# Copying the rows of a key and value cache inside DRAM, instead of storing them from the tiles that were loaded for the attention

## The chip, the cores and the metric

The kernel is one program on one NeuronCore of one Trainium2 chip. The metric is device time in microseconds (us); a row of the profile is one execution of that program as the hardware profiler saw it. The engines are called as the profile calls them: PE (TensorE, matmuls), PEld (its weight loads), DVE (VectorE), ACT (ScalarE), POOL (GpSimd), SP (SyncE). SP, ACT and POOL issue DMAs, each on a ring of its own (q1, q10 and q0 in the profile); all rings are served by the same 16 DMA engines. SPq is SP's queue as an issuer of DMAs.

## The reference, cut to what matters

One inference step of one decoder layer: a prompt of 1024 tokens and, beside it, 8 sequences of 8 new tokens each with a cache of 2048 rows of keys and values (8 heads of 64, so 512 floats or 2 KB a row). A mixer of two head groups (gated DeltaNet and windowed attention) is followed by a SwiGLU FFN. For the 8 sequences, the attention reads the cache and the step also returns the cache moved on by 8 rows:

```python
def token_mix(h, conv_buf, s0, win_k, win_v, ...):
    proj = h @ w_in
    ...
        n_past = win_k.shape[1]                                    # 2048
        kc = jnp.concatenate([win_k.astype(kb.dtype), kb], axis=1)
        vc = jnp.concatenate([win_v.astype(vb.dtype), vb], axis=1)
        parts = [dilated_branch_sample(qf, kcf, vcf, slopes, d, w // d, n_past) for (w, d) in DILATED]
        keep = min(MAX_WINDOW, n_past + T)                         # 2048
        new_k, new_v = kc[:, n_past + T - keep:], vc[:, n_past + T - keep:]
    o_b = rmsnorm(combine_by_denominator(parts), norm_out_b)
    mixed = jnp.concatenate([o_a.reshape(B, T, A_WIDTH), o_b.reshape(B, T, B_WIDTH)], axis=-1)
    return mixed @ w_out, new_conv, s_new, new_k, new_v

def hybrid_block(x, ...):
    mix, new_conv, new_rec, new_k, new_v = token_mix(rmsnorm(x, norm_mix), ...)
    x = x + mix
    hf = rmsnorm(x, norm_ffn)
    x = x + (jax.nn.silu(hf @ w_gate) * (hf @ w_up)) @ w_down
```

So `new_wk_sample[b, 0:2040] = cache_win_k[b, 8:2048]`, its last 8 rows are the new keys, and the same holds for V. That is 2040 rows of 2 KB for each of 8 sequences, for K and for V. The attention itself reads only a part of the cache: with a dilation of 16 the first eight of every 16 rows of rows 0 to 1535, and all of the last 512 rows.

## The kernel before

All matmuls of the dense parts are made exact by splitting both operands into a high and a low part, so each weight block costs three matmuls. A weight block of 128 x 1024 floats is loaded by SP into `wraw` (two buffers, `WB`), ACT copies the high part into `whi`, DVE takes the low part into `wlo` (three buffers each, `WH` and `WL`; `wsplit` and `split`, L216 to L233).

The program is written as Python generators that record the work of a stage and yield a cost; `beside` (L1384) takes from a main stage and, by a pace given as a number, from one or two stages beside it. The Tile framework then schedules the recorded instructions for each engine by their dependences and priorities, so an engine's final order differs from the order of recording; each engine runs its own order and waits on semaphores. `tc.keep_in_program_order` pins an instruction to its recorded place.

The stages in order: the projection `proj_a` of both halves of the prompt with the DeltaNet `gdn` beside it (its small block copies into `N1` run on POOL, L650 and L651), `proj_b` with the first half of `decode_k` (`dk`, attention scores of the 8 sequences against the cached keys) beside it, the attention of the prompt `attn(0)` and the output projection `outproj_a`; then the dense work of the first half of the prompt (`outproj_b(0)`, `ffn(0)`) with `attn(1)`, the second half of `decode_k` and then `decode_v` beside it; last `out1` and `ffn(1)` for the second half.

`decode_k` works on pairs of sequences. For each sequence it loads the last 512 rows in two tiles `kt` of 512 KB (L1021; transposed by PE, copied to `kaT` by ACT, multiplied with the query block `qbd`), and the 16-dilated rows in four tiles of 384 KB (L1037; multiplied on DVE with a broadcast query `qbc`, the product `pr`, L994). `kt` has three buffers. `decode_v` loads the values likewise into `vt` (four buffers, L1104) and splits them into `vh` and `vl`. In both, each loaded tile is stored from SBUF into the moved cache by a DMA that POOL issues (L1022, L1038, L1107, L1109):

```python
sp.dma_start(kt[:96], c16[:96, t:t + 2])
pool_q.dma_start(o16[0:95, 8 + t:10 + t], kt[1:96])
scores(S[:, s, t * 8:t * 8 + 16], kt[:96], q[:96], 96)
```

A buffer of `kt` or `vt` may be loaded anew only when its store has landed. The rows that the attention doesn't read (the second eight of every 16) are copied inside DRAM by `far_rows`, one DMA of 96 pieces of 16 KB (1536 KB) for each sequence, on SP's queue, pinned to its recorded place: for K beside `proj_b(0)`, for V beside `out1` and `ffn(1)`.

Of the kernel before, what the change touches and what calls it, by code (L numbers as in the profile page):

```python
# [22 lines left out]
DB, DS = 8, 8  # L23
PAST = 2048
# [7 lines left out]
R1 = 2.0  # L32
# [5 lines left out]
R7 = 1.4  # L38
# [7 lines left out]
U3 = 120  # L46
# [94 lines left out]
def body(tc, I, O, C, off):  # L141
# [843 lines left out]
    def decode_k(tp, pairs, kb=2, kt_=3, qb=2, pb=1):  # L985
# [23 lines left out]
        for pi in pairs:  # L1009
            S = tp.tile([96, 2, 64], F32, name="S", tag="S", bufs=1)  # L1010
            pa = obank()
            for s in range(2):
# [6 lines left out]
                for r in range(0, 4, 2):  # L1019
                    kbt = tp.tile([128, 2, 512], F32, name="kt", tag="kt", bufs=kt_)  # L1020
                    sp.dma_start(kbt, c4[:, r:r + 2])  # L1021
                    pool_q.dma_start(o4[:, r:r + 2], kbt)  # L1022
                    for q in range(2):
                        p_ = nbank()
                        for j in range(4):
                            pe.transpose(p_[:, j * 128:(j + 1) * 128], kbt[:, q, j * 128:(j + 1) * 128], ident)
                        kaT = tp.tile([128, 4, 128], F32, name="kaT", bufs=kb)
                        act.activation(kaT, p_.rearrange("p (j m) -> p j m", j=4), AF.Copy)
                        for j in range(4):
                            mm(pa[s * 64:(s + 1) * 64, (r + q) * 128:(r + q + 1) * 128], qbd[:, s, j], kaT[:, j],  # L1030
                               j == 0, j == 3)
                    yield 4.0
                for t in range(0, 8, 2):
# [4 lines left out]
                    pool_q.dma_start(o16[0:95, 8 + t:10 + t], kt[1:96])  # L1038
# [19 lines left out]
    def decode_v(tp):  # L1058
# [10 lines left out]
        for pi in range(4):  # L1069
# [17 lines left out]
            for s in range(2):  # L1087
# [11 lines left out]
                for i in range(6):  # L1099
# [6 lines left out]
                    if i < 4:  # L1106
                        pool_q.dma_start(o16[0:95, 8 + 2 * i:10 + 2 * i], vt[1:96])  # L1107
                    else:
                        pool_q.dma_start(o4[:, 2 * i - 8:2 * i - 6], vt)  # L1109
# [228 lines left out]
    def far_rows(c, o, new):  # L1338

        for b in range(DB):  # L1340
            c16, o16, *_ = cache_rows(c, o, b)
            tc.keep_in_program_order(sp.dma_start(o16[0:96, 0:8], c16[0:96, 8:16]))
            yield 4.5
# [91 lines left out]
    far = Side(far_rows(I["cache_win_k"], O["new_wk_sample"], smp[1]))  # L1435
    beside(Side(proj_a(1, tpa, tp, *acts1)), (gd, R0))
    tst2.close()
    beside(Side(proj_b(0, tp, *acts0)), (gd, R1), (far, 0.3))
    far.run()
# [29 lines left out]
    with ExitStack() as s1:  # L1469
        at1 = Side(attn(1, pool(s1, "at", "right"), **A1), ahead=O4)  # L1470
        beside(dense, (at1, R7), until=U3)
        at1.run()
    pst.close()
# [17 lines left out]
    far = Side(far_rows(I["cache_win_v"], O["new_wv_sample"], smp[2]))  # L1491
    beside(out1, (far, 0.3))
    beside(Side(ffn(1, op, x2, hp)), (far, 0.3))
# [28 lines left out]
```

## Time and profile before

| what | value |
|---|---|
| time, median of 3 runs | 1830.91 us (1815.8 to 1832.13) |
| profiled execution | 1808.45 us, of it 1806.7 us span from the first to the last instruction |
| mean granted clock of PE in it | 0.982 |
| busy share of the span | PE 95%, PEld 82%, DVE 64%, ACT 38%, POOL 5% |
| moved by DMA | 325.00 MB; on SP's ring 275.64 MB, on POOL's ring 43.08 MB |

The profiled execution lies 1.2% under the median of the runs, so changes are added up against its own time. The share of a busy engine is an average over stages: what a change is worth is read in the stage where it acts. A DMA share of 1 means that all 16 DMA engines were busy. A wait in brackets names what the engine was released by.

### The profile page before, as it was taken

What the parts mean: (1) busy time and instruction counts of PE and PEld (TensorE: products, weight loads), DVE (VectorE), ACT (ScalarE), POOL (GpSimd) and SP (SyncE); (2) the same over time, 40 slices, a digit from 0 to 9 for tenths busy, and PEclk for the clock granted to TensorE, in tenths of its full rate; (3) what the DMA queues carried; (4) which work ended last, traced back from release to release, by engine and by line L of the source; (5) the groups of instructions that cost most, each with busy time, mean ns of one, the idle gap of its engine ahead of it and who ended that gap; (6) DMA issues with size and microseconds to landing.
All of it is one profiled execution on the core that took longest, in us unless ns stands there. A gap on an engine that the chain in (4) does not pass through costs nothing. (4 is left out here: it accounts for less than half of the span.)

```text
span 1806.7 us, 28517 instructions
## 1 busy us (share of the span) xinstructions
PE 1716.0 (95%) x10718; PEld 1490.3 (82%) x10718; DVE 1151.8 (64%) x2829; ACT 695.3 (38%) x1411; POOL 84.7 (5%) x208
## 2 busy tenths in 40 slices
PE   6999999998999999999998899999997999999997
PEld 6988799987656668978977787788887999999996
DVE  7879776866775657897655556676576444353445
ACT  5545344442333444676422234444234222131222
POOL 0000000001001000000010201111100000000000
PEclk9999999999999999999999999999998999999999
DMA  6444555558987957633288859898395332241321
GB/s 204 130 141 129 152 192 142 176 180 278 294 246 250 284 172 240 211 103 104 79 265 247 258 159 325 250 293 275 123 330 171 132 103 82 59 130 38 112 71 64
DMA packets 305476, 325.00 MB, mean 180 GB/s; under 512 B 28349, under 2 KB 252605, under 8 KB 303786
## 3 DMA queue, kind: packets, MB, share of 16 engines
q1 hardware_dynamic: 291610, 275.64, 50.3%
q0 software_dynamic: 12352, 43.08, 6.9%
q10 hardware_dynamic: 1376, 4.46, 0.6%
q8 instruction: 84, 1.38, 0.3%
q14 instruction: 54, 0.44, 0.1%
HBM read 242.92 MB, written 105.63 MB: 193 GB/s over the span
## 5 line engine op out<-in xcount | busy, mean ns | idle before, releaser
L192 PE MATMUL pm<-act_hi,whi 128*128 128x288 f32 (+1 forms) x1056 | 351.4, 333 | 0.7 <-DVE hth L1294 0.4
L192 PE MATMUL pm<-act_lo,whi 128*128 128x288 f32 (+1 forms) x1056 | 350.8, 332 | 0.0
L192 PE MATMUL pm<-act_hi,wlo 128*128 128x288 f32 (+1 forms) x1056 | 349.5, 331 | 0.0
L217 ACT ACTIVATE whi<-wraw 128x1024 fp32r<-128x1024 f32 x182 | 192.9, 1060 | 354.0 <-PE pm L192 257.6
L218 DVE TENSOR_TENSOR wlo<-wraw,whi 128x1024 fp32r<-128x1024 f32 x182 | 222.4, 1222 | 120.0 <-ACT whi L217 119.4
L192 PE MATMUL pm<-xh,whi 128*128 128x320 f32 (+2 forms) x672 | 229.0, 341 | 4.6 <-DVE th L424 2.7
L192 PE MATMUL pm<-xh,wlo 128*128 128x320 f32 (+2 forms) x672 | 228.3, 340 | 0.6 <-DVE wlo L218 0.5
L192 PE MATMUL pm<-xl,whi 128*128 128x320 f32 (+2 forms) x672 | 227.7, 339 | 0.1
L192 PEld LDWEIGHTS pm<-act_hi,whi 128*128 128x128 f32 x1056 | 200.8, 190 | 17.5 <-issue 1.5
L192 PEld LDWEIGHTS pm<-act_lo,whi 128*128 128x128 f32 x1056 | 200.8, 190 | 15.3 <-issue 1.3
L192 PEld LDWEIGHTS pm<-act_hi,wlo 128*128 128x128 f32 x1056 | 200.7, 190 | 14.7 <-issue 0.7
L192 PEld LDWEIGHTS pm<-xh,whi 128*128 128x128 f32 x672 | 129.3, 192 | 16.2 <-DVE th L424 2.9
L1319 DVE TENSOR_TENSOR x<-pm,x 128x256 f32<-128x256 f32 (+1 forms) x148 | 79.9, 544 | 94.3 <-PE pm L192 93.9
L192 PEld LDWEIGHTS pm<-xh,wlo 128*128 128x128 f32 x672 | 129.0, 192 | 11.7 <-DVE wlo L218 1.6
L192 PEld LDWEIGHTS pm<-xl,whi 128*128 128x128 f32 x672 | 128.9, 192 | 11.5 <-issue 2.7
L192 PE MATMUL pm<-own,hh 128*128 128x512 f32 x440 | 129.4, 390 | 0.0
L192 PE MATMUL pm<-whi,hh 128*128 128x256 f32 (+1 forms) x336 | 99.3, 297 | 5.3 <-DVE x L1319 3.3
L192 PE MATMUL pm<-whi,hl 128*128 128x256 f32 (+1 forms) x336 | 97.4, 292 | 0.0
L192 PE MATMUL pm<-wlo,hh 128*128 128x256 f32 (+1 forms) x336 | 97.2, 290 | 0.0
L192 PEld LDWEIGHTS pm<-own,hh 128*128 128x128 f32 x440 | 82.2, 188 | 16.9 <-issue 0.2
L192 PE MATMUL pm<-whi,nat_hi 128*128 128x256 f32 x288 | 83.4, 294 | 2.0 <-DVE n_ss L213 1.1
L1292 ACT ACTIVATE hth<-pm 128x288 f32<-128x288 f32 (+1 forms) x66 | 30.5, 462 | 139.7 <-PE pm L192 139.7
(365 smaller groups left out, 3248.4 us busy)
## 6 DMA issues: line engine op xcount, KB each, us to landing
wraw<-w_in SPq DMA_DIRECT2D x56, 512.0 KB, 4.9
wraw<-w_gate SPq DMA_DIRECT2D x44, 512.0 KB, 4.2
wraw<-w_up SPq DMA_DIRECT2D x44, 512.0 KB, 3.7
wraw<-w_down SPq DMA_DIRECT2D x44, 512.0 KB, 3.7
new_wk_sample<-cache_win_k SPq DMA_DIRECT2D x8, 1536.0 KB, 9.1
qbc<-smp SPq DMA_DIRECT2D x32, 384.0 KB, 5.4
kt<-cache_win_k SPq DMA_DIRECT2D x32, 384.0 KB, 6.1
vt<-cache_win_v SPq DMA_DIRECT2D x32, 384.0 KB, 4.3
```

The lines of the kernel that those rows point to most:

```text
L192: pe.matmul(out, lhsT, rhs, start=start, stop=stop)
L217: act.activation(hi, src, AF.Copy)
L218: dve.tensor_sub(lo, src, hi.bitcast(F32))
L1292: act.activation(th, pg[:, :n], AF.Tanh, scale=0.5)
L1319: dve.tensor_tensor(xv, ps, xv, op=OP.add)
```

## The change

The four stores out of `kt` and `vt` are taken out of `decode_k` and `decode_v`. `far_rows` becomes `move_rows`: for each sequence two DMAs, from DRAM to DRAM, of 1020 consecutive rows each (2.09 MB), which together are all 2040 rows. They are issued on POOL's queue instead of SP's and are no longer pinned. K is recorded beside `proj_b(0)` and the dense work beside `attn(1)`, V beside `ffn(1)`. The loads for the attention stay as they are.

```diff
--- before.py
+++ after.py
@@ -1019,7 +1019,6 @@
                 for r in range(0, 4, 2):
                     kbt = tp.tile([128, 2, 512], F32, name="kt", tag="kt", bufs=kt_)
                     sp.dma_start(kbt, c4[:, r:r + 2])
-                    pool_q.dma_start(o4[:, r:r + 2], kbt)
                     for q in range(2):
                         p_ = nbank()
                         for j in range(4):
@@ -1035,7 +1034,6 @@
                     q_rows(q[:96], t, b, 96)
                     kt = tp.tile([128, 2, 512], F32, name="kt", tag="kt", bufs=kt_)
                     sp.dma_start(kt[:96], c16[:96, t:t + 2])
-                    pool_q.dma_start(o16[0:95, 8 + t:10 + t], kt[1:96])
                     scores(S[:, s, t * 8:t * 8 + 16], kt[:96], q[:96], 96)
                     yield 3.0
             p_ = nbank()
@@ -1103,10 +1101,6 @@
                     vl = tp.tile([128, 2, 512], F32R, name="vl", bufs=VB)
                     sp.dma_start(vt[:n], c16[:96, 2 * i:2 * i + 2] if i < 4 else c4[:, 2 * i - 8:2 * i - 6])
                     split(vh[:n], vl[:n], vt[:n])
-                    if i < 4:
-                        pool_q.dma_start(o16[0:95, 8 + 2 * i:10 + 2 * i], vt[1:96])
-                    else:
-                        pool_q.dma_start(o4[:, 2 * i - 8:2 * i - 6], vt)
                     for q in range(2):
                         mm(po, z[:n, 2 * i + q], vh[:n, q], i + q == 0, False)
                         mm(po, z[:n, 2 * i + q], vl[:n, q], False, False)
@@ -1335,12 +1329,15 @@
                         yield nb * ncol / 800
             f += nb
 
-    def far_rows(c, o, new):
-
+    def move_rows(c, o, new):
+
+        n = (PAST - DS) // 2
         for b in range(DB):
-            c16, o16, *_ = cache_rows(c, o, b)
-            tc.keep_in_program_order(sp.dma_start(o16[0:96, 0:8], c16[0:96, 8:16]))
-            yield 4.5
+            for q in range(2):
+                s_, d_ = (x[0, b, r:r + n].rearrange("(a e) h d -> a (e h d)", a=60) for x, r in
+                          ((c, DS + q * n), (o, q * n)))
+                pool_q.dma_start(d_, s_)
+                yield 4.5
         sp.dma_start(o[0, :, PAST - DS:PAST].rearrange("b t h d -> b t (h d)"), new.rearrange("(b t) f -> b t f", t=DS))
 
     def steps(*gens):
@@ -1432,11 +1429,10 @@
     nc.gpsimd.memset(Bz, 0.0)
     nc.gpsimd.memset(N1, 0.0)
     gd = Side(gdn(gp, Bz, N1), gdn_sample(gp), ahead=O1)
-    far = Side(far_rows(I["cache_win_k"], O["new_wk_sample"], smp[1]))
+    far = Side(move_rows(I["cache_win_k"], O["new_wk_sample"], smp[1]))
     beside(Side(proj_a(1, tpa, tp, *acts1)), (gd, R0))
     tst2.close()
-    beside(Side(proj_b(0, tp, *acts0)), (gd, R1), (far, 0.3))
-    far.run()
+    beside(Side(proj_b(0, tp, *acts0)), (gd, R1), (far, 0.2))
     es0.close()
     pst.close()
     psum(pst, m=2, n=2, g=2, c=1, o=1)
@@ -1468,8 +1464,9 @@
     dense = Side(outproj_b(0, hp, x2), ffn_norm(0, hp, x2), ffn(0, hp, x2, hp))
     with ExitStack() as s1:
         at1 = Side(attn(1, pool(s1, "at", "right"), **A1), ahead=O4)
-        beside(dense, (at1, R7), until=U3)
+        beside(dense, (at1, R7), (far, 0.25), until=U3)
         at1.run()
+        far.run()
     pst.close()
     psum(pst, **PSE)
     with ExitStack() as s1:
@@ -1488,9 +1485,9 @@
     pst.close()
     psum(pst, m=6, n=2)
     hp = pool(st0, "hh")
-    far = Side(far_rows(I["cache_win_v"], O["new_wv_sample"], smp[2]))
-    beside(out1, (far, 0.3))
-    beside(Side(ffn(1, op, x2, hp)), (far, 0.3))
+    far = Side(move_rows(I["cache_win_v"], O["new_wv_sample"], smp[2]))
+    beside(out1)
+    beside(Side(ffn(1, op, x2, hp)), (far, 0.22))
     far.run()
     st0.close()
     st1.close()
```

The program that is built from it has another order. At the start of the program, POOL's order was this (`gdn_S`, `Bz` and `N` are buffers of the DeltaNet, `N` is `N1` of the code):

```order
L1422 MEMSET gdn_S 128x512
L1432 MEMSET Bz 128x1024
L1433 MEMSET N_1431 128x512
L650 COPY N_1431<-L 32x4x32
L651 COPY N_1431<-L 32x4x32
```

Now there are copies between them:

```order
L1419 MEMSET gdn_S 128x512
L1339 DMA new_wk_sample<-cache_win_k 32x16320 x3
L1429 MEMSET Bz 128x1024
L1430 MEMSET N_1431 128x512
L1339 DMA new_wk_sample<-cache_win_k 32x16320 x3
L650 COPY N_1431<-L 32x4x32
L651 COPY N_1431<-L 32x4x32
L1339 DMA new_wk_sample<-cache_win_k 32x16320 x3
```

Nine of the 16 K copies stand at the first three places of POOL's order, recorded a stage or more later.

On POOL again, from the end of the first half of `decode_k` over `outproj_a` (`xq` is its residual tile) to the second half of `decode_k` (`qbd`), it was:

```order
L1038 DMA new_wk_sample<-kt 95x1024 x4
L1204 MEMSET xq 64x256 x2
L1055 DMA pd<-Pd 128x616
L1204 MEMSET xq 64x256 x2
L1007 MEMSET qbd 128x512
L1018 COPY qbd<-qf 64x8 x16
L1022 DMA new_wk_sample<-kt 128x1024 x2
```

And now:

```order
L1339 DMA new_wv_sample<-cache_win_v 32x16320 x2
L1198 MEMSET xq 64x256
L1339 DMA new_wv_sample<-cache_win_v 32x16320
L1053 DMA pd<-Pd 128x616
L1198 MEMSET xq 64x256 x2
L1339 DMA new_wv_sample<-cache_win_v 32x16320
L1198 MEMSET xq 64x256
L1339 DMA new_wv_sample<-cache_win_v 32x16320 x5
L1007 MEMSET qbd 128x512
L1018 COPY qbd<-qf 64x8 x32
```

The last V copy stands ahead of the second half of `decode_k`, two stages before the one in which it was recorded; the stores are gone from their places behind `qbd`.

On SP, at the entry into `out1` and `ffn(1)` (`wffn` is the norm's weight row), it was:

```order
L222 DMA wraw<-w_out 128x4x256 x2
L1342 DMA new_wv_sample<-cache_win_v 96x4096
L222 DMA wraw<-w_out 128x4x256
L294 DMA wffn<-norm_ffn 128x1024
L1342 DMA new_wv_sample<-cache_win_v 96x4096
L222 DMA wraw<-w_gate 128x8x128
L222 DMA wraw<-w_up 128x8x128
L1342 DMA new_wv_sample<-cache_win_v 96x4096 x2
```

And now:

```order
L222 DMA wraw<-w_out 128x4x256 x2
L294 DMA wffn<-norm_ffn 128x1024
L222 DMA wraw<-w_out 128x4x256
L222 DMA wraw<-w_gate 128x8x128
L222 DMA wraw<-w_up 128x8x128
```

The copies between the weight loads are gone from SP's order.

## Rows read from the trace of the kernel before

**Rows 1.** Page, busy time of each engine, share of the span and instructions

```profile
PE 1716.0 (95%) x10718; PEld 1490.3 (82%) x10718; DVE 1151.8 (64%) x2829; ACT 695.3 (38%) x1411; POOL 84.7 (5%) x208
```

**Rows 2.** Stretches: length, then busy us (instructions) by engine, granted clock, DMA share, GB/s

```profile
3.00:15.00 12.00, 4.11 (x17) 3.38 (x17) 8.30 (x26) 6.79 (x12) 0.00 (x0) 1.00 0.96 322
29.00:60.00 31.00, 31.00 (x224) 31.00 (x225) 29.59 (x83) 19.64 (x41) 1.42 (x2) 0.93 0.47 125
130.00:160.00 30.00, 30.00 (x173) 25.01 (x173) 27.03 (x104) 18.25 (x54) 0.57 (x2) 1.00 0.42 125
206.50:211.00 4.50, 2.91 (x25) 2.61 (x24) 2.99 (x7) 2.05 (x3) 0.00 (x0) 0.97 0.94 390
400.00:520.00 120.00, 108.33 (x624) 82.67 (x623) 86.83 (x230) 37.74 (x102) 11.63 (x32) 1.00 0.89 272
520.00:700.00 180.00, 174.86 (x968) 122.83 (x968) 110.62 (x315) 75.20 (x186) 11.81 (x33) 0.99 0.76 235
700.00:760.00 60.00, 56.17 (x424) 51.77 (x423) 45.70 (x118) 31.38 (x61) 0.31 (x1) 1.00 0.73 230
900.00:1060.00 160.00, 142.92 (x820) 120.85 (x820) 84.94 (x106) 37.72 (x52) 21.67 (x57) 0.96 0.81 242
1060.00:1300.00 240.00, 234.99 (x1277) 197.21 (x1276) 152.65 (x228) 102.39 (x139) 29.19 (x58) 0.99 0.79 250
1300.00:1400.00 100.00, 89.00 (x572) 80.61 (x571) 68.40 (x164) 37.42 (x58) 2.87 (x5) 0.91 0.68 239
```

**Rows 3.** Stretches at the lower clock between 900 and 1300, same columns

```profile
937.80:944.60 6.80, 5.80 (x17) 4.70 (x18) 3.58 (x4) 0.95 (x2) 0.52 (x1) 0.50 0.90 278
1036.80:1043.60 6.80, 3.01 (x10) 2.07 (x10) 4.20 (x5) 1.60 (x3) 0.38 (x1) 0.50 0.72 202
1118.70:1125.50 6.80, 5.81 (x13) 4.12 (x14) 5.12 (x5) 3.24 (x4) 1.05 (x2) 0.50 1.08 381
```

**Rows 4.** Waits of SP's DMA queue: us in total, times, longest us

```profile
SPq L1037 <- DMA new_wk_sample<-kt: 49.6, 15, 7.2
SPq L1104 <- DMA new_wv_sample<-vt: 48.1, 18, 5.2
```

**Rows 5.** Timeline around 1033: start us, us, engine, line, operation [idle before <-releaser]

```profile
1026.30 0.53 POOL L1038 DMA_DIRECT2D new_wk_sample<-kt  x1 [0.56 <-DMA kt<-cache_win_k]
...
1032.04 0.31 SPq L1037 DMA_DIRECT2D kt<-cache_win_k  x1
...
1036.23 1.22 DVE L994 TENSOR_TENSOR pr<-kt,qbc 96x1024 f32<-96x1024 f32 x1 [6.26 <-DMA kt<-cache_win_k]
...
1040.59 0.66 PE L192 MATMUL po<-kaT,qbd 128*64 128x128 f32 x2 [7.82 <-ACT kaT L1028]
```

**Rows 6.** Timeline of POOL, same columns

```profile
0.74 0.53 POOL L1422 MEMSET gdn_S<- 128x512 f32 x1 [0.29 <-POOLq L1513]
33.66 0.96 POOL L1432 MEMSET Bz<- 128x1024 f32 x1 [32.40 <-DVE n_ss L208]
...
138.56 0.28 POOL L650 COPY N<-L 32x128 f32<-32x128 f32 x1 [103.48 <-DVE L L556]
...
702.44 0.31 POOL L1204 MEMSET xq<- 64x256 f32 x1 [7.19 <-DMA k<-ks]
```

**Rows 7.** Timeline of the start, same columns

```profile
8.99 1.28 DVE L283 SCALAR_TENSOR_TENSOR xn<-xt,n_ss,wmix 128x1024 f32<-128x1024 f32 x1 [0.52 <-DMA wmix<-norm_mix]
...
10.50 1.06 ACT L217 ACTIVATE whi<-wraw 128x1024 fp32r<-128x1024 f32 x1 [3.50 <-DMA wraw<-w_in]
```

**Rows 8.** Instructions on y_prompt: time from DMA to landing

```profile
DMA to landing us min/median/max: 2.0/6.0/6.0
```

**Rows 9.** Old copies into new_wk_sample: ns min/median/max of an issue, first and last start

```profile
L1342 SPq DMA_DIRECT2D new_wk_sample<-cache_win_k x8: 517/591/663, 203.7 to 430.1; - x8
```

**Rows 10.** DMA issues, 1334 to 1366: queue, count, KB each, us to landing

```profile
new_wv_sample<-cache_win_v SPq DMA_DIRECT2D x3, 1536.0 KB, 11.2
y_prompt<-xn ACTq DMA_DIRECT2D x3, 512.0 KB, 6.0
```

## The prediction, made before the changed kernel ran

> **What bounds the kernel now.** I read the busy shares first: TensorE (PE) has 95% of the span, every other engine far less [rows 1], so only what stops PE, or keeps its clock low, can be won or lost. The table by stage [rows 2] shows where PE stands idle: 17.1 us of the 160 us from 900 to 1060 (the second half of the K decode beside the first FFN), 11.7 us from 400 to 520 (the first half of the K decode), 5.1 from 520 to 700, 3.8 from 700 to 760, 5.0 from 1060 to 1300 (the V decode), 11.0 from 1300 to 1400. The decode stages are those with DMA engines 76 to 89% busy. Three stretches of 6.8 us in them ran at a granted clock of 0.50 [rows 3], the lower of TensorE's levels (1.2 instead of 2.4 GHz); each begins at an idle gap of PE.
>
> Then I asked what the idle time hangs on. SP's queue waited 49.6 us at the `kt` loads for stores out of the same buffers and 48.1 us at the `vt` loads for theirs [rows 4]. The timeline at the longest gap shows the mechanism [rows 5]: a store leaves `kt` at 1026.30, the next `kt` load is issued only at 1032.04, VectorE (DVE) stands 6.26 us in its own queue for a late `kt` and multiplies at 1036.23; behind that stand `hth` and ScalarE's `kaT`, and PE resumes at 1040.59 after 7.82 us. So the stores out of `kt` cost PE time although nobody reads their result: they hold the buffer.
>
> **Where the work goes.** Removed: 64 stores of 380 KB and 32 of 512 KB (41.7 MB) and 16 copies of 1536 KB (25.2 MB) on SP's ring. Added: 32 copies of 32 x 16320 floats (2.09 MB each, 66.8 MB) on GpSimd's (POOL's) ring. The bytes that DMA engines move stay the same; their time and place don't. One old copy alone moved in about 4.5 us, with everything beside it at 390 GB/s [rows 2]; at that rate a new one takes 5.4 us (estimate: 2.09 MB / 390 GB/s), three in a row 16 us, five 27.
>
> The source paces the V copies into the second FFN, but POOL's order in the built program doesn't keep that: the copies wait for no tile and the scheduler has them up front. Three stand right behind the `gdn_S` memset, at 0.74 us; three behind the `Bz` and `N1` memsets, at 33.66; three behind the first copies into `N1`, at 138.56; seven more K copies singly and in pairs behind the later ones; four V copies behind the first `qbd` copies, three behind `kq`, then two, one, one, and five behind the last `xq` memset at 702.44 [rows 6]. By about 740 everything would be copied. I call that the built schedule and work with it.
>
> **Start, 0 to 29 us: cost.** The start is bound by loads: from 3 to 15 us the DMA engines are 96% busy [rows 2], `xn` waits for `wmix` until 8.99 and `whi` for its weights until 10.50 [rows 7]. Three copies now fall into just that stretch. If both rings get equal turns, loads run at half rate from about 3.3 us on (2 us from issue to the first packet; a store that landed soonest took 2.0 [rows 8]): `wmix` is 5.7 us later, the weights 7.2. Ends: 0, if copies take only what is left over, and +16, if all three go first. I take +7, the equal share.
>
> **Bursts of three near 34 and 139 us: small.** PE is busy 31.0 of 31 us and 30.0 of 30 there, the DMA engines 47% and 42% [rows 2]: 16 us of copying fit beside it. At equal turns loads lose at most 8 us of engine time in each burst; weights are held two finished tiles ahead (`WH` = `WL` = 3), which hides most. Ends 0 and +8 each; I take +1 each, by the idle half of the engines.
>
> **Single copies, 204 to 431 us: nothing.** Eight copies of 1.57 MB inside SP's ring [rows 9], where loads queue behind them, become seven of 2.09 MB beside it. SP's ring loses what POOL's gains; 0, ends -4 and +4. The other work of PE there hides both; if that cover were gone, one copy would cost its 5.4 us.
>
> **First K decode and attention, 400 to 760 us: a cost.** Sixteen V copies bring 33.4 MB, 86 us of all engines at 390 GB/s. Out go the stores of four batches (10.4 MB, 27 us) and two of the old copies (8 us): 51 us more. Idle engine time there is 13 + 43 + 16 = 72 us [rows 2], so it fits on average but not in each burst: the five copies behind 702.44 last 54 us at equal turns, in which the loads want 73% (39 us) and get 27, so 12 us come late. Against that stands that `kt` is no longer held by stores here either, with 11.7 us of PE idle to win from. Ends -8 and +20; I take +6, the late 12 us half hidden.
>
> **Second K decode and V decode, 900 to 1300 us: the gain.** Here stores go and nothing comes. To be won: 17.1 + 5.0 us of idle PE, and the 14.62 us of PE work done at half clock [rows 3] would take half, 7.3 less: 29 us together. What is late next: `qbc`, which is loaded per step with two buffers, and the order on DVE itself. I take 70%, -21; ends -28 and -8 (the longest gap alone).
>
> **Behind it, 1300 to 1400 us.** The old V copies leave SP's ring and the weights of the second FFN come sooner, but the idle PE there stands behind a row of norms on DVE (68 of 100 us busy) [rows 2]. I take -1, ends -6 and 0.
>
> **Sum.** +7 +2 +0 +6 -21 -1 = -7 us. It is made against the profiled execution (1806.7 us span, 1808.45 with what lies around it). That execution was 1.2% faster than the median of the runs, 1830.91; I put the difference on the median: 1824 us. All low ends together give -46, all high ends +48; 8 in 10 I put at -35 to +31.
>
> **Rivals.** (a) *The copies give way.* Loads and copies interleave so finely that latency hides the copies: start +2, bursts 0, 400 to 760 -6 (the `kt` loop relieved, the copies in the gaps), then -24 and -2. That is -30: 1801 us. For it: from 1334 to 1366, beside old copies of 1536 KB and weights, a store of 512 KB from another ring still landed in 6.0 us [rows 10] against 2.0 at the shortest for a store of `y_prompt` [rows 8]. Against it: 96% busy at the start leaves no room to hide in.
>
> (b) *The copies hold the engines, and it gets slower.* If an engine finishes each large packet of a copy before it turns to the other ring, a load of many small packets waits for all copies issued near it. Start +16, bursts of three +5 each, 400 to 760 +18, then -18 and -1: +25, 1856 us. It decides from the point where start and bursts together cost more than 22 us. For it: one old copy kept the engines 94% busy [rows 2]; against it the 6.0 us of [rows 10], which leave little room for waiting in turn. The Trainium skill, page "DMA: Bandwidth & Descriptors", section "Queues, rings and completion order", speaks against this change: each DMA engine goes round the rings packet by packet and finishes a packet before it switches. By that rule all three first copies would be served before the first weights, and the sum would be this rival's. The row of the store at 6.0 us doesn't settle it, since the old copies' rows were 16 KB pieces and the new ones are up to 64 KB.
>
> (c) *The decode's idle time isn't the stores'.* The order on DVE keeps the gaps, only the SP wait goes: -6 instead of -21, and +7 +2 +6 -1 stand: +8, 1839 us. For it: PE also idles behind DVE's norms without any DMA. Against it: the buffer is named as what is waited for [rows 4, 5].
>
> (d) *The change doesn't do what it says.* If POOL stood still at a wait for an earlier copy's end (the program lets eight be under way), copies into `N1` and `qbd` behind it would hold PE. At 5.4 us each the ninth copy, at 139 us, finds the first long landed; I give it no time of its own and count it in (b).
>
> **How the numbers follow.** Chances: forecast 0.42, (a) 0.29, (b) with (d) 0.20, (c) 0.09. The runs before lie 0.9% apart, so 1% (18 us) is about what can be told from no change. Faster by over 1% are (a) and a little of the forecast's lower side: 0.33. Slower: (b) and a little of the forecast's upper side: 0.23. Within: 0.44. The likeliest case's own range is 1808 to 1840; the range reaches to both sides' rivals, 1796 to 1862.
>
> **What would show it.** Right: PE idle from 900 to 1300 falls from 22 us to under 8 and the half-clock stretches there are gone; the first weights are split at 16 to 19 us instead of 10.50; waits of SP's queue for `new_wk_sample` and `new_wv_sample` are gone; DMA share under 0.65 from 900 to 1300. Wrong: first weights before 12 us or after 24; idle gaps of PE over 5 us around 140 or 710; decode gaps that stay with `kt` landed. A schedule whose PE order is worse elsewhere, since all orders were made anew, would make the forecast wrong without any of this.

## The result, and the profile after

The changed kernel takes 1959.63 us (median, 1951.53 to 1963.94) against 1824.94 us before (1815.80 to 1832.13) on the same chip: a ratio of 1.0752, 95% interval 1.0710 to 1.0793. It is 135 us slower. The prediction, 1824 us with a range of 1796 to 1862, was wrong (its base, 1830.91, lies 6 us above the 1824.94 measured here). The profiled execution after took 1951.53 us, its span is 1949.7 us; before it was 1808.45 and 1806.7.

From the page of the changed kernel, the busy times, the DMA queues (packets, MB, share of 16 engines) and the copies (KB each, median us to landing):

```profile
PE 1750.8 (90%) x10718; PEld 1517.4 (78%) x10718; DVE 1152.3 (59%) x2829; ACT 696.4 (36%) x1411; POOL 49.9 (3%) x144
...
q1 hardware_dynamic: 289818, 250.47, 43.7%
q0 software_dynamic: 2112, 68.24, 9.9%
...
new_wk_sample<-cache_win_k POOLq DMA_DIRECT2D x16, 2040.0 KB, 13.1
```

PE has the same number of instructions as before [rows 1] and is busy 35 us longer, at a mean granted clock of 0.945 instead of 0.982. The other 108 us by which the span grew are idle time of PE. A K copy lands 13.1 us after its issue in the median, where 2.09 MB at the 390 GB/s of [rows 2] would take 5.4. SP's loads went as 289818 packets of 864 bytes on the average. Each of POOL's copies goes as its 32 rows, in packets of 65 KB (65280 bytes).

The stages of the changed kernel, columns as in [rows 2] (a packet counts whole in the window in which it starts, so a DMA share can pass 1). Behind the start, the same work lies 17 to 169 us later than before; 1069 to 1443 answers to 900 to 1300 of before, 1450 to 1550 to about 1307 to 1407:

```profile
3.00:15.00 12.00, 0.00 (x0) 0.00 (x0) 2.40 (x16) 2.30 (x4) 0.00 (x0) 1.00 1.16 438
...
52.00:80.00 28.00, 21.55 (x167) 21.34 (x165) 17.99 (x53) 12.47 (x27) 1.61 (x4) 0.97 0.97 305
166.00:192.00 26.00, 16.37 (x94) 13.61 (x93) 14.13 (x45) 11.72 (x44) 1.99 (x5) 0.85 0.91 291
400.00:520.00 120.00, 91.17 (x526) 78.33 (x524) 87.14 (x285) 33.74 (x103) 8.21 (x24) 0.88 0.79 234
...
832.00:876.00 44.00, 12.13 (x90) 11.43 (x90) 8.84 (x15) 5.04 (x7) 2.65 (x6) 0.66 0.95 317
...
1060.00:1300.00 240.00, 236.37 (x1379) 201.93 (x1378) 151.44 (x218) 81.25 (x112) 7.84 (x37) 1.00 0.67 194
1069.00:1443.00 374.00, 370.08 (x2090) 313.21 (x2089) 237.29 (x331) 139.66 (x190) 9.69 (x41) 1.00 0.62 180
1450.00:1550.00 100.00, 89.64 (x584) 81.79 (x584) 70.04 (x169) 37.90 (x58) 0.95 (x1) 0.93 0.44 145
```

The rows from 1060 to 1300 and 1069 to 1443 are the gain that was forecast: behind the last copy PE is idle 3.9 us in 374, at the full clock. The last row is the stage in which next to nothing was forecast. The rows ahead of these are the loss: in the short stretches, which follow a burst of copies, the DMA engines are 91 to 116% busy and PE is idle for a fifth of the time or more. Two of these places in the timeline, the start and the five V copies at 832 (columns as in [rows 5]):

```profile
3.20 21.27 SPq L328 DMA_DIRECT2D xt<-x_prompt  x2
...
26.51 1.28 DVE L283 SCALAR_TENSOR_TENSOR xn<-xt,n_ss,wmix 128x1024 f32<-128x1024 f32 x1 [18.17 <-DMA wmix<-norm_mix]
...
28.43 1.06 ACT L217 ACTIVATE whi<-wraw 128x1024 fp32r<-128x1024 f32 x1 [21.57 <-DMA wraw<-w_in]
...
832.37 2.42 POOL L1339 DMA_DIRECT2D new_wv_sample<-cache_win_v  x5 [0.15 <-issue]
...
874.72 0.80 PE L192 MATMUL ps<-kst,qh 128*128 128x512 f32 x1 [31.87 <-ACT qh L217]
```

`xn` and `whi` come 17.5 and 17.9 us later than before [rows 7]; SP itself stands 21.27 us at the issue of two loads. The copies at 832 are followed by one gap of 31.87 us on PE. The waits of PE in total, times, longest:

```profile
PE pn L288 <- DVE xn L283: 41.1, 6, 27.8
PE ps L192 <- ACT qh L217: 31.9, 1, 31.9
PE pg L192 <- DMA Bz<-xd: 21.5, 1, 21.5
PE pc L192 <- DVE rhs L688: 15.9, 3, 9.2
```

The third of them, `Bz<-xd`, will turn out to be there without the copies' bytes, too. The waits of SP for `new_wk_sample` and `new_wv_sample` [rows 4] are gone from the view.

### The profile page after: what moved, and what is told of

It is laid out like the page before. It is cut to its first block, busy times and chain, and to the rows that moved or that the text cites. A ratio compares the mean times of both kernels' runs of the same rounds, so it can differ in the third digit from the quotient of the medians.

```text
span 1949.7 us, 28333 instructions
## 1 busy us (share of the span) xinstructions
PE 1750.8 (90%) x10718; PEld 1517.4 (78%) x10718; DVE 1152.3 (59%) x2829; ACT 696.4 (36%) x1411; POOL 49.9 (3%) x144
## 3 DMA queue, kind: packets, MB, share of 16 engines
q1 hardware_dynamic: 289818, 250.47, 43.7%
## 5 line engine op out<-in xcount | busy, mean ns | idle before, releaser
L217 ACT ACTIVATE whi<-wraw 128x1024 fp32r<-128x1024 f32 x182 | 192.9, 1060 | 473.9 <-PE pm L192 346.2
L192 PEld LDWEIGHTS pm<-xh,whi 128*128 128x128 f32 x672 | 130.5, 194 | 17.9 <-DVE th L424 5.8
L192 PE MATMUL pm<-wlo,nat_hi 128*128 128x256 f32 x288 | 84.5, 298 | 0.0
## 6 DMA issues: line engine op xcount, KB each, us to landing
new_wk_sample<-cache_win_k POOLq DMA_DIRECT2D x16, 2040.0 KB, 13.1
```

The lines of the kernel that those rows point to most:

```text
L192: pe.matmul(out, lhsT, rhs, start=start, stop=stop)
L217: act.activation(hi, src, AF.Copy)
```

## The experiments

Three theories were held against each other. **Theory 1:** each DMA engine goes round the rings packet by packet, so loads in small packets all but stand still while copies in large ones are under way. **Theory 2:** the orders of all engines, made anew by the Tile framework around the copies, are worse in themselves. **Theory 3:** the bytes cost their time at these places, whatever the packets. "Later" below is the difference of the ends of the same matmul (same output, operands and count) in two traces.

### Are the copies' bytes the loss, or the order around them?

**tiny_copies.** The changed kernel with each copy moving only 16 of the 16320 floats of each of its rows, so that nearly no bytes are left.

```diff
-                pool_q.dma_start(d_, s_)
+                pool_q.dma_start(d_[:, 0:16], s_[:, 0:16])
```

> The changed kernel with each copy moving 16 of the 16320 floats of each row (the other cache rows are left out of the output): the 32 issues stay on POOL at about their places, 66.7 of 66.8 MB of the copies go. Theory 1 and 3 (the copies cost the time by what they move): 1770 to 1800 us, below the kernel before, since the stores out of kt and vt are gone as well; PE starts before 12 us. Theory 2 (orders): 1900 or more.

Measured: 1798.46 us, ratio 0.9876 (0.9828 to 0.9924). The expectation was wrong on the place: all 32 short copies were issued between 1.3 and 23.3 us, and the order on PE differs from the changed kernel's in 2312 of 10718 places. The time is right for theories 1 and 3, but it doesn't exclude theory 2, since the framework counted the copies as short. What it does show is the gain without its cost. Against the kernel before, the same matmuls end 12.4 us later at 934 (this new order loses its time between 420 and 480) and 12.3 us earlier at 1174: 24.7 us won in the second K decode and the V decode. The changed kernel itself shows the same gain: its matmuls end 168.8 us later than before at 1060 and 143.3 later at 1300, so 25.5 us are won between.

**two_rows and two_small.** These have the changed kernel's order on all five engines (two matmuls of 10718, three places apart, are exchanged), with 1/16 of the bytes: two rows of each copy, as they are, or two short pieces out of each of 16 parts; the shapes are such that the framework counts a copy as long as before.

```diff
-  x[0, b, r:r + n].rearrange("(a e) h d -> a (e h d)", a=60)
+  x[0, b, r:r + n].rearrange("r h d -> (r h d)").rearrange("(a f) -> a f", a=32)[0:32:31]             # two_rows
+  x[0, b, r:r + n].rearrange("r h d -> (r h d)").rearrange("(m a e) -> a m e", a=32, m=16)[0:32:31]   # two_small
```

> The changed kernel with each copy moving 2 of its 32 rows of 16320 floats (the other cache rows are left out of the output); the order on all five engines is the changed kernel's, instruction by instruction. Theories 1 and 3 (traffic): 1790 to 1805 us, as in the run with tiny copies. Theory 2 (order): 1900 or more. Between them, the part above 1798 is the order's.

> The changed kernel's orders on all five engines, each copy moving 2 x 16 pieces of 4080 bytes, 1/16 of its bytes (the other cache rows are left out of the output). What this is above 1798 is the order's alone: if order, 1855 to 1875; if the 75 us that the run with two long rows had left were their packets on single DMA engines, 1800 to 1815. PE starts before 12 us either way.

Measured: 1873.05 us (1.0259, 1.0222 to 1.0296) and 1858.40 us (1.0204, 1.0153 to 1.0254). So neither theory 2 nor the traffic is the whole loss. The two rows of 65 KB cost 15 us more than the same bytes in 32 pieces. The order, with the sixteenth of the bytes that is left, makes 60 us: 1858 against 1798. Some 3 us of this stand at the start and may be those bytes' (weights first split at 13.46 instead of 10.56). The traffic makes 101 us more by the medians, 1960 against 1858, and 90 by the profiled executions, since that of the changed kernel is the fastest of its four. PE's busy time, from the pages of tiny_copies and two_small:

```profile
PE 1719.5 (96%) x10718; PEld 1494.3 (83%) x10718; DVE 1152.5 (64%) x2829; ACT 696.2 (39%) x1411; POOL 48.3 (3%) x144
PE 1741.7 (94%) x10718; PEld 1511.3 (81%) x10718; DVE 1152.8 (62%) x2829; ACT 696.7 (37%) x1411; POOL 53.8 (3%) x144
```

So of the order's 65.5 us of span, 22 are the same matmuls taking longer (mean granted clock 0.959 instead of 0.981) and 43 idle time of PE; of the traffic's 89.9 they are 9 and 81. Most of the changed kernel's loss at the lower clock therefore comes with the order. The waits of PE in two_small show a part of it:

```profile
PE pg L192 <- DMA Bz<-xd: 21.3, 1, 21.3
PE pn L288 <- DVE xn L283: 17.1, 4, 12.9
PE pn L1171 <- DMA mt<-mix: 8.3, 1, 8.3
```

The gap of 21.3 us at `Bz<-xd` is there almost without traffic; in tiny_copies the same wait is 1.4 us. Up to 300 us the projection's matmuls run 15.7 us ahead of those in tiny_copies; then they are used up, and PE has nothing beside the chain of `Xblk` steps on DVE that leads to `Bz`. At 525 they are 25.9 us later, at 805 us 64.0. The 38 us between weren't followed to single waits: from 600 to 810 PE is idle 24 us, at a granted clock of 0.86.

Where the traffic's part arises, changed kernel against two_small:

| end in the changed kernel, us | later by, us | what lies between |
|---|---|---|
| 32 | 13.7 | three copies at the start |
| 57 to 84 | 14.2 to 23.7 | three copies at 52 |
| 159 to 191 | 22.8 to 33.1 | three copies at 167 |
| 216 to 419 | 34.2 to 40.4 | six single or in pairs |
| 419 to 809 | 40.4 to 65.1 | eleven, at most three together |
| 809 to 898 | 65.1 to 93.4 | one at 818, five at 832 |
| to the end | 92 to 90 | none |

### Is it the size of the packets?

**small_pieces.** The changed kernel with each copy written as pieces of 1020 floats (4080 bytes); bytes and orders stay.

```diff
-  .rearrange("(a e) h d -> a (e h d)", a=60)
+  .rearrange("r h d -> (r h d)").rearrange("(m a e) -> a m e", a=32, m=16)
```

> The changed kernel with each copy cut into pieces of 1020 floats (4080 bytes) instead of rows of 16320 floats; same bytes, and the orders of all five engines stay as in the changed kernel, place by place. Turns by packet (theory 1): a load then waits for some 4 KB of a copy at each turn and no longer for 64 KB, wmix lands before 16 us instead of 26, and most of the 135 us loss comes back: 1820 to 1870 us. The orders made anew are worse in themselves (theory 2): 1940 to 1965, unchanged. Sheer bytes at these times (theory 3): 1930 to 1965, start unchanged.

Measured: 1961.03 us (1.0766, 1.0711 to 1.0820), as slow as the changed kernel, which by the time alone was theory 3's number. Theory 1's first sign came, `wmix` was there by 15.45 instead of 26.51, but the first weights were split only at 31.14. The pieces were merged in pairs: its page has 9280 packets on POOL's ring, 7168 more than the changed kernel, which is 224 more for each of the 32 copies, so 256 of 8160 bytes. The window from 6 to 20 us shows what the engines served, POOL's ring (q0) and SP's (q1), packets and MB. First the changed kernel:

```profile
q0 software_dynamic: 96, 4.18, 83.3%
q1 hardware_dynamic: 99, 0.41, 8.6%
```

Then small_pieces:

```profile
q0 software_dynamic: 473, 3.73, 80.6%
q1 hardware_dynamic: 470, 0.95, 21.5%
```

The engines serve as many packets of the one ring as of the other, 96 and 99, 473 and 470 (short ones included: 32 packets of the first window, all of them POOL's, and 48 of the second are under 512 bytes). The same holds under the five V copies: while the `k` loads, of 128 KB each in rows of 1 KB, wait, the window from 840 to 864 of the changed kernel has 189 to 187:

```profile
q0 software_dynamic: 189, 8.29, 103.6%
q1 hardware_dynamic: 187, 0.19, 2.4%
```

That is theory 1's mechanism, a packet for a packet: 24 us bring 8.29 MB of copies and 0.19 MB of loads. The Trainium skill, page "DMA: Bandwidth & Descriptors", section "Queues, rings and completion order", says that each engine goes round the queue rows packet by packet; these counts agree. But the shares of bytes follow from the packets on both sides, and 0.95 MB instead of 0.41 doesn't help a start that needs 3.5 MB (four `xt`, `tab`, `wmix` and the first `wraw`, of 0.5 MB each): all but the end of the three copies lands first either way.

**start_three and start_three_small.** The kernel before, with three copies added behind the `gdn_S` memset and nothing moved; start_three_small writes them as pieces of 4080 bytes.

```diff
+    scr = [dp.tile([60, 8704], F32, name=f"scr{i}") for i in range(3)]
+    for i in range(3):
+        pool_q.dma_start(scr[i], I["cache_win_k"][0, i, 8:1028].rearrange("(a e) h d -> a (e h d)", a=60))
```

> The kernel before with three copies of 32 x 16320 floats added right behind the gdn_S memset on POOL, cache rows into scratch in DRAM; nothing else is changed and the orders stay. Theory 1: +17 us (1842), PE starts at about 27.5 us. Equal share of bytes, as predicted: +7. Theory 2: at most +7.

> The same three added copies in pieces of 1020 floats (4080 bytes). Theory 1: turns of about equal size, +5 to +9 us, PE starts at 16 to 19 us. Theory 3 (bytes alone, whatever the pieces): +17 as with the large ones.

Measured: 1838.57 us (1.0085, 1.0052 to 1.0117) and 1840.24 us (1.0103, 1.0039 to 1.0166). In start_three PE starts at 28.64 us; the window shows 98 packets of copies beside 102 of loads. So the start's share is the copies' own, without any new order: 17 us by the medians (10 to 21 by the interval). The smaller pieces bring PE's first transposes forward to 16.77, as theory 1 said, but the first weights are split at 30.51 instead of 28.74, and the time doesn't change, against theory 1's number and for the reason above.

**start_act.** The same with `act.dma_start` in place of `pool_q.dma_start`.

> The kernel before with the three added copies (32 rows of 65280 bytes) at the start on ScalarE's queue instead of POOL's: another ring, whose packets are made in another way. If any second ring takes its turn packet by packet: +11 to +17 us, in a window with both rings full as many packets of each and 0.4 to 0.6 MB of loads in 14 us. If it was POOL's ring in particular: 0 to +5.

Measured: 1828.06 us (1.0057, 1.0018 to 1.0097), short of the expected loss. ACT's own work parts the copies, the first at 0.75, the second at 16.82, and PE starts at 15.50 instead of 10.33: 5.2 us for one copy. So it isn't POOL's ring in particular; a burst of three puts PE's start off by 18.3 us, a single one by 5.2. While the first copy is in flight, from 4.5 to 8.5 us, ACT's ring and SP's get 16 packets each. (The orders differ a little from the kernel before, in 57 places on PE.)

**Rows with gaps: row_pieces, start_three_rows, start_act_rows.** Every second row of the cache per copy, meant to keep every piece at 2048 bytes.

```diff
+  x[0, b, r:r + 2 * n].rearrange("(m a two) h d -> two a m (h d)", two=2, a=34)[q]
```

> The changed kernel with each copy taking every second cache row, so that no two rows lie side by side and a piece can't be longer than one row of 2048 bytes; same bytes, same number of copies, at nearly the same places on POOL. Turns by packet (theory 1): loads in packets of 4096 bytes now get two thirds of the bytes in each turn, wraw lands before 20 us instead of 28, the time falls to 1830 to 1880 us. Bytes alone (theory 3): the loads lose as much as with 65 KB and 8 KB pieces, wraw lands after 24 us, 1930 to 1975 us.

> The kernel before with the same three added copies at the start in rows of 2048 bytes with gaps between; the orders of all engines are those of the other two kernels with three added copies. Theory 1: +4 to +8 us (1826 to 1830), PE starts before 20 us. Theory 3: +17 us, PE starts after 26 us.

> The same on ScalarE's queue in rows of 2048 bytes with gaps between, so that POOL's writing of pieces, which held the copies back to 57 us in the run with rows on POOL, plays no part. Turns by packet: loads get half or more of the bytes, PE starts at its 10.3 us, +3 to +8 us. Bytes alone, whatever the packets: as with long rows on the same queue, +11 to +17.

Measured: 2352.76 us (1.2909), 1877.87 us (1.0303) and 1922.84 us (1.0561). All three times missed, for a reason of their own: the copies became slow. Theory 1's signs did come: in start_three_rows PE starts at 10.31 us, as it does before, and in row_pieces the first weights are split at 17.95, ahead of the 20 named. But a copy lands after 57.0 us, and POOL, which has the copy to issue, stands 51 us before the third. On ACT's ring an eighth of the engines' time is used, and the profile names the copy as what a load of SP waits for. The timeline of POOL in start_three_rows:

```profile
1.38 6.00 POOL L1425 DMA_DIRECT2D scr<-cache_win_k  x2
58.68 2.91 POOL L1425 DMA_DIRECT2D scr<-cache_win_k  x1 [51.29 <-issue]
```

The window from 20 to 50 us in start_act_rows, and its wait of SP's queue, in two fences:

```profile
DMA packets 737, 1.54 MB, mean 51 GB/s; under 512 B 4, under 2 KB 4, under 8 KB 737
...
q10 hardware_dynamic: 716, 1.47, 12.5%
```

```profile
SPq L328 <- DMA scr<-cache_win_k: 43.8, 1, 43.8
```

The 12.5% are the time of two of the 16 engines. Gaps alone aren't shown to be the cause: the shape changed too (34 pieces in its first dimension instead of 32), and copies in 4 KB pieces with gaps land within 12.0 to 14.5 us on the same ring in act_late, below. The signs fit theory 1, but copies that bring so little in a microsecond leave room for loads whatever the turns, so nothing more is taken from these runs.

### Would the copies be free elsewhere?

**pin_sp and pin_sp_two_rows.** The copies on SP's queue, kept in program order: K beside the projection and the first FFN, V in the second FFN.

```diff
-                pool_q.dma_start(d_, s_)
+                tc.keep_in_program_order(sp.dma_start(d_, s_))
```

> The changed kernel with the copies on SP's queue and kept in program order: the K copies follow the projection and the first FFN as written, the V copies the second FFN, one at a time among SP's loads. Theories 1 and 3 (the loss is where and in what bursts POOL's ring moves the bytes): 1790 to 1815 us, PE starts before 12 us. Theory 2 (all orders made anew are worse): above 1850.

> The kernel with the copies in order on SP's queue (1926 us), each moving 2 of its 32 rows, all orders as there. If that kernel's loss is the order built around copies that the program's planner takes to be long: 1890 to 1930. If it is traffic: 1790 to 1810.

Measured: 1926.09 us (1.0578, 1.0547 to 1.0609) and, with 1/16 of the bytes and the same orders, 1912.95 us (1.0487, 1.0440 to 1.0533). Theories 1 and 3 gave 1790 to 1815; they missed by over 100 us. All but 13 us of this kernel's loss stays when the bytes go, save for what two packets of 65 KB a copy cost beside the same bytes in small ones (15 us in two_rows).

**fine_sp, fine_late and fine_late_two_rows.** Copies a quarter as long, four times as many, at the same places, or all in the second FFN.

```diff
-        n = (PAST - DS) // 2
...
+        n = (PAST - DS) // 8
...
+                tc.keep_in_program_order(sp.dma_start(d_, s_))
+                yield 4.5 / 4
```

> The kernel with the copies kept in order on SP's queue (1926 us), each copy cut into four of 0.52 MB in time: 128 copies spread over the same stretches of the program. A load of weights behind one copy then waits some 2 to 3 us instead of 8 to 12, which two weight tiles ahead hide. If the loss of that kernel is the wait of single loads behind one long copy: 1800 to 1840 us, and the second FFN loses under 15 us instead of 57. If it is the bytes: 1900 to 1940.

> The same 128 copies of 0.52 MB on SP's queue, all of them paced into the second FFN, behind both decodes (66.8 MB in some 420 us). If single waits were the loss: 1785 to 1825 us, at or below the kernel before, with the stages up to 1400 us as in the kernel whose copies move almost nothing (1798). If bytes are: the second FFN loses 100 us and more, 1890 to 1930.

> The kernel with 128 copies in the second FFN (1902 us), each moving 2 of its 16 rows, all orders as there: the splits of weights on DVE stand behind the additions to x. If the order is its loss: 1880 to 1905. If traffic: 1790 to 1810.

Measured: 2119.27 us (1.1648), 1902.16 us (1.0458, 1.0402 to 1.0514), and with 1/8 of the bytes 1904.25 us (1.0434, 1.0402 to 1.0466). fine_late is the kernel without copies up to 1369 us (within 6 us of tiny_copies) and loses 100 us behind it; its twin, with the same orders, loses as much, so this is order (but for what the twin's own long packets cost). Why fine_sp is slowest of all wasn't followed further: against tiny_copies it loses 102 us up to 800, another 121 up to 1300 and some 98 in the second FFN, like fine_late; for the first two there is no twin.

**mid_late.** All bytes in the second FFN again, in gapped pieces of 16 KB like the old copies.

```diff
+                s_, d_ = (x[0, b, r:r + PAST - DS].rearrange("(m a) h d -> m (a h d)", a=8)[q::4]
+                          for x, r in ((c, DS), (o, 0)))
```

> All 66.8 MB on SP's queue in the second FFN, as 64 copies of 1.05 MB, each of 64 pieces of 16 KB with gaps between them as the old copies had. The splits on DVE then stand where they stood before. Theory 1 (a copy costs where loads wait behind it, and one or two at a time are covered by weights two tiles ahead): 1790 to 1815 us, faster than both kernels or as fast as the one before. Theory 3 (bytes cost their time wherever they go): 1880 to 1960.

Measured: 1858.23 us (1.0202, 1.0151 to 1.0252), between the two expectations. Its timeline shows how an order costs time here:

```profile
1500.16 1.06 ACT L217 ACTIVATE whi<-wraw 128x1024 fp32r<-128x1024 f32 x1 [1.68 <-DMA wraw<-w_up]
...
1505.71 0.69 DVE L1313 TENSOR_TENSOR x<-pm,x 128x512 f32<-128x512 f32 x1 [0.89 <-PE pm L192]
1506.32 2.35 DVE L218 TENSOR_TENSOR wlo<-wraw,whi 128x1024 fp32r<-128x1024 f32 x2
...
1507.59 0.40 PE L192 MATMUL pm<-act_hi,wlo 128*128 128x288 f32 x1 [1.65 <-DVE wlo L218]
```

In tiny_copies the same step stands ahead of the additions to `x`:

```profile
1456.94 1.23 DVE L218 TENSOR_TENSOR wlo<-wraw,whi 128x1024 fp32r<-128x1024 f32 x1 [0.42 <-ACT whi L217]
1458.08 0.68 DVE L1313 TENSOR_TENSOR x<-pm,x 128x512 f32<-128x512 f32 x1
```

In mid_late the weights are there and `whi` is done at 1501.2, but DVE's order has `wlo` behind all additions to `x`, which wait for PE; so PE runs dry, here for 1.65 us. Such waits for `wlo` come to 16.3 us in the second FFN, 15 of them, where tiny_copies has none; they are a part of the 63 us that mid_late loses there. That the framework, which counts the copies ahead of the loads on SP's queue, takes the weights to come late is argued from the orders and from fine_late_two_rows, and not shown.

**thin2_late and act_late.** 32 copies in gapped pieces of 4 KB, which the framework counts as short. The order on PE is the same in both and differs from that of tiny_copies in 118 of 10718 places; thin2_late has the copies on SP's queue (one of them at 365 us), act_late on ACT's.

```diff
+                s_, d_ = (x[0, b, r:r + PAST - DS].rearrange("(m a) h d -> m (a h d)", a=2)[q::2]
+                          for x, r in ((c, DS), (o, 0)))
+                tc.keep_in_program_order(sp.dma_start(d_, s_))      # act.dma_start in act_late
```

> All 66.8 MB on SP's queue in the second FFN, as 32 copies of 2.09 MB, each of 510 pieces of 4 KB with gaps between them; the order on PE is, instruction by instruction, the one of the changed kernel with its copies taken out, and DVE's differs in 24 places. If the order is what the copies in the second FFN cost (1858 and 1902 us in the two runs before): 1780 to 1815 us, faster than the kernel before or as fast. If the traffic: 1850 or more.

> The kernel with 32 copies of 2.09 MB in pieces of 4 KB in the second FFN, issued by ScalarE instead of SP; the orders of PE and SP are, row by row, those of the kernel without copies. If rings take turns packet by packet, a load of 4 KB packets beside 4 KB pieces is at most about half as fast, some 2 us later, which weights held ahead cover: 1795 to 1825 us, at or a little below the kernel before, and the second FFN loses under 25 us instead of 80. If it is the traffic itself, or ScalarE standing at its own issues: 1850 or more.

Measured: 1879.67 us (1.0334, 1.0295 to 1.0373) and 1940.88 us (1.0676, 1.0635 to 1.0717). Both expectations for the good case missed. With the order so nearly held, the traffic costs some 80 us in the second FFN, though the DMA engines are nearly idle for long stretches. The window from 1505 to 1520 in thin2_late:

```profile
DMA packets 334, 0.18 MB, mean 12 GB/s; under 512 B 13, under 2 KB 333, under 8 KB 333
```

SP's queue stands at a load there whose buffer isn't free (its waits for `hth` at L222 come to 185.4 us in this stage, the longest 26.3), and the copy, which waits for nothing, stands behind that load in SP's order. It is issued just when loads are needed again. act_late shows what a second ring does then. From its page, KB each and us to landing:

```profile
wraw<-w_gate SPq DMA_DIRECT2D x44, 512.0 KB, 6.4
wraw<-w_up SPq DMA_DIRECT2D x44, 512.0 KB, 11.7
wraw<-w_down SPq DMA_DIRECT2D x44, 512.0 KB, 7.3
```

and the waits of PE and ACT in the second FFN:

```profile
PE pm L192 <- ACT hh L1289: 110.3, 8, 15.1
...
ACT own L217 <- DMA wraw<-w_down: 133.9, 17, 12.3
```

A load of `w_up` lands in 3.8 us in tiny_copies. My expectation had taken loads to be 4 KB packets. They aren't; the window from 1600 to 1640 in tiny_copies has weight loads alone:

```profile
q1 hardware_dynamic: 5200, 2.62, 22.6%
```

That is 504 bytes a packet: a row of a 128-column weight tile is 128 floats. A load of 512 KB is some 1024 packets, a copy in 4 KB pieces 510. At one packet each by turns nearly the whole copy has landed before half of the load has. The trace has it so: from 1610 to 1616, behind the issue of a `w_up` load at 1607.81 and of a copy at 1605.47, ACT's ring (q10) and SP's get

```profile
q10 hardware_dynamic: 339, 1.36, 87.1%
q1 hardware_dynamic: 321, 0.16, 10.1%
```

With pieces of 8 or 65 KB a copy has still fewer packets than a load: by these counts that is why the size of the pieces made so little difference from 65 KB down to 4 KB. ACT then stands in its own order at `own` for the late `w_down`, and `hh`, and PE, behind it. ACT's own issues are not the cause: they took 0.83 us each, some 27 us for all 32. No version found here beats the kernel before with all rows copied.

## Why the prediction was wrong, point by point

- **The step that failed** is "If both rings get equal turns, loads run at half rate ... I take +7, the equal share", and with it the price of every burst. Turns are equal in packets (96 to 99), not in bytes (4.18 to 0.41 MB). A load of many small packets waits until nearly all copies in flight have landed. Rival (b) said so and had 0.20.
- **Start:** +7 forecast, +16 as its upper end. Measured 13.7 us against the same order, 17 in start_three. First weights at 28.43 us, beyond the 24 named as wrong.
- **Bursts of three:** +1 each, upper end +8. Measured 9.5 and 10.3 us. They were said to fit beside PE's work, since the engines were only 47% and 42% busy [rows 2]. Free engine time over the stretch didn't help the loads that came behind a burst.
- **Singles:** 0, ends -4 and +4; measured 6 us for six, a little beyond.
- **400 to 760:** +6, upper end +20. Measured 25 and 28 us, 53 together; the five copies were expected to leave 12 us of loads late, half hidden. They left `k` loads of 128 KB landing after 33 us and PE idle for 31.87.
- **The gain, 900 to 1300:** -21 forecast. Right, and a little small: 25.5 us in the changed kernel, 24.7 in tiny_copies; PE idle 3.9 us from 1069 to 1443, the half-clock stretches of [rows 3] gone, the DMA share 0.62, as the prediction's signs said. So rival (c), that the idle time wasn't the stores', falls.
- **1300 to 1400:** -1; the row at 1450 after, 89.64 of 100, answers to the 89.00 of [rows 2]. Right.
- **Rival (b)** had the mechanism, but its price was too low, +25: bursts at +5 instead of 10, 400 to 760 at +18 instead of 53. It priced the copies' transfers and not what stands behind them in the orders of SP, ACT and DVE. With the measured sizes it is about 1807 - 25 + 14 + 20 + 6 + 53 = 1875 in the profiled time.
- **Rival (d)** falls: POOL issued the five copies at 832 in 2.42 us, without a wait.
- **The term that wasn't there** is the rest, some 75 us: the order made anew, 65.5 us of span by two_small against tiny_copies (60 by the medians) and the 12.4 us that tiny_copies itself loses before 934. The prediction named it in its last sentence as something that could make it wrong, without a price or a chance.

The account in spans: 1806.7 before; -12.4 with the stores gone and the copies counted as short (24.7 won, some 12.4 lost to that order); +65.5 for the order around long copies (1859.8 of two_small against 1794.3 of tiny_copies); +89.9 for their traffic: 1949.7.

What stays open: how the 53 us of 400 to 898 divide between the late loads and the half clock behind each gap; which waits make up the order's loss between 525 and 805; and fine_sp's loss ahead of the second FFN.

## What to carry to other kernels

Ask of a transfer that is to run "beside" loads not whether the engines have free time, but how many packets of it stand between a load and its landing: with rings served packet by packet, a load of 1024 packets waits for nearly the whole of a copy that has fewer, however large these are, and the buffers held ahead must cover that. Where a scheduler makes the order, an added long transfer has a second price, the new order, and it can be measured apart: keep the shape that the scheduler counts, and take the bytes out. Here stores that held a buffer were cheaper than every version of copies that held none; that this is because a store starts when its tile is there, and a copy whenever its queue is free, is argued and not shown.

## What the runs showed of the hardware that was not expected

- While both had work, two rings got as many packets each, whatever their sizes: 96 to 99, 98 to 102, 473 to 470 in 14 us, 189 to 187 in 24 us, 339 to 321 in 6 us.
- A row of a weight tile, 512 bytes, is a packet of its own (504 bytes on the average), while neighbouring pieces of a copy are merged (4080 bytes given, 8160 moved).
- SP stood 21.27 us at the issue of two loads, while its ring hardly moved (99 packets, 0.41 MB in 14 us), and issued nothing behind them.
- Copies of 2 KB rows with gaps, in the shape used here, were slow: 51 GB/s in the window on ACT's ring, at 12.5% of the engines' time, and 57 us to landing on POOL's against 16.7 for the same bytes in long rows. Copies of 4 KB pieces with gaps, in another shape, landed in 12.0 to 14.5 us on ACT's ring.
